# One layer of a hybrid attention and convolution trunk: the first two FFN groups' up products in another order around the last token tile, and one tile's block sums and one weight fetch a tile later

## The chip, the cores and the metric

The kernel runs on one core of a Trainium2 chip. The metric is device time in microseconds (us) of one execution, the median of several runs.

## The reference

One layer over 1024 tokens of 1024 channels, everything in float32. What matters here is the end of the mixer and the start of the feed-forward part:

```
m = sigmoid(g_att) * y_att + sigmoid(g_conv) * y_conv
x = x + rms_norm(m @ w_out, norm_mix_post)              # output projection
h = rms_norm(x, norm_ffn_pre)
a, g = split(causal_dwconv3(h @ w_up, conv_ffn_w))      # w_up: 1024 x 5632
x = x + rms_norm((gelu_tanh(g) * a) @ w_down, norm_ffn_post)
```

## The kernel before, in words

All matrix products run in float16 pairs: a float32 operand is split into a high and a low half (ACT writes the high half, L97, and VectorE the low half, L98), and three passes high·high, high·low and low·high are added up in PSUM. Before a weight is split, a power-of-two scale is made from its sum of squares: ACT squares it (L58, tile `jk_u2_0` for the first weight of group 2), VectorE reduces and casts (L70, L71), TensorE adds over partitions with a matrix of ones (L76, tile `pr`), and VectorE turns the result into the scale (L78 to L81, tile `sc`).

**Output projection** (mixer, L1112 to L1192). It goes over eight token tiles tt of 128 tokens. For each, `out_proj(tt)` issues 48 matmuls of 128x512 on PE (L1123, two PSUM banks `py`); ACT squares each bank for the norm (L1125, `jk_n_post`), VectorE takes it out (L1126, `hn`), then follow the row factor (L181 on VectorE, a power on POOL L182), the residual `x2` (L1130) and its write to memory by SP (L1131), a second square sum on ACT (L58, `jk_n_ffn`), again L181 and L182, and L1133 writes the normed row tile `hn`. The x rows `xr` come in by SP (L1176), one tile ahead, into a pool of 4 buffers that is shared with the raw FFN weights `ws_u`.

**Block sums** (`blocks(tt, h)`, L1136 to L1171). PE transposes `hn` in 8 steps into two banks `pt` (L1141). For tiles 0 to 3, ACT and VectorE only split them into `hA` (L1149, L1150). For tiles 4 to 7 they also build sums and differences of the four 512x512 blocks of h (L1155 to L1167, tiles `tb`, `hb`, into `hA` and `hB`).

**Up products** (class `Pair`). Each of the 22 groups f has the columns of w_up for 128 channels of a and of g. A 2x2 block product is done with seven block products instead of eight (a Strassen form), from four weight tiles `wh_u` and the blocks of hA and hB. `prod(i)` issues 12 matmuls of 128x512 (L1538) into one of three banks, and `evict` takes the sum out. Products 1 and 2 share bank a: product 1 is taken out by ACT (L1553, `cgu`), and product 2 adds on top of it in the same bank and is taken out as `cau` (L1603). Products 6, 7, 4 share bank b (L1555, L1562, L1567 on VectorE), products 5 and 3 bank c (L1558 on ACT, L1565 on VectorE). After product 3 and 4 come the convolutions (L1612 to L1615), the gelu (L1622) and the product `ua` (L1623).

```
    A = {1: (0, 0), 2: (0, 1), 3: (3, 0), 4: (1, 1), 5: (2, 0), 6: (2, 1), 7: (1, 0)}
        ...
        bank = {1: "a", 2: "a", 5: "c", 3: "c"}.get(i, "b")
        first = i in (1, 6, 5)
        if first:
            self.ps[bank] = l.bank(f"p{self.name}{bank}")
        ...
        with l.tc.high_priority():
            self.evict(i, ps)
```

Products 1 and 2 read hA of tokens 0 to 511 (tiles 0 to 3) alone. Products 5, 6 and 7 read hB, and products 3 and 4 the second half of hA, so they need the block sums of tile 7. `pu0a` is bank a of group 0, `pu1c` bank c of group 1, and so on.

**What sets the order.** The program is written in one order, and a scheduler of the framework moves instructions on each engine by its own simulated times, with priority for `evict` and, in the first two groups, for `blocks(7)`. PSUM is one pool of 8 banks. Engines execute their own instructions strictly in the resulting order. `pair_fetch` issues the two transfers of a group's weights and the square sums on ACT; `pair_sums` and `pair_split` build and split the four weight tiles (L1233 to L1248, L97, L98). The down product of FFN groups 0 and 1 (`pd`, L1312) needs the split gelu output `f16` and w_down tiles `wd`, which SP fetches (L1275) into the same pool of 4 raw weight buffers once a `ws_u` is split.

Of the kernel before, what the change touches and what calls it, by code (L numbers as in the profile page):

```python
# [39 lines left out]
class Layer:  # L40
# [235 lines left out]
    def mixer(self, mid):  # L276
# [716 lines left out]
        with ExitStack() as ph2:  # L993
# [8 lines left out]
            def blocks(q):  # L1002
                lo, hi = ds(0, NH), ds(NH, NH)
                kA, kB = ds(2 * q, 2), ds(KH + 2 * q, 2)

                def diff(name, p, m, hT_m=True):

                    t = self.slot([P, 2, NH], F32, f"{name}_{q}")
                    nc.vector.tensor_tensor(t, hT[:, 0, p[0], p[1]], hT[:, 0, m[0], m[1]] if hT_m else m,
                                            ALU.subtract)  # L1010
                    nc.vector.tensor_tensor(t, t, hT[:, 1, p[0], p[1]], ALU.add)
                    if hT_m:
                        nc.vector.tensor_tensor(t, t, hT[:, 1, m[0], m[1]], ALU.subtract)
                    return t
                t1 = diff("T1", (kA, hi), (kA, lo))
                halves(hB[:, :, 0, ds(2 * q, 2), :], t1)
                t2 = diff("T2", (kB, hi), t1, False)
                halves(hB[:, :, 1, ds(2 * q, 2), :], t2)
                t4s.append(diff("T4", (kB, lo), t2, False))
                t3 = diff("T3", (kB, hi), (kA, hi))  # L1020
                halves(hB[:, :, 2, ds(2 * q, 2), :], t3)
# [91 lines left out]
        def out_proj(tt):  # L1113
            xt = xr.pop(tt)
            sm = self.small(f"r_post{tt}")
            h = self.slot([P, D], F32, f"hn{tt}")
            jk = self.junk(f"jk_n_post{tt}")
            for nh in range(2):
                ps = self.bank(f"py{tt}_{nh}")
                sl = ds(nh * NH, NH)  # L1120
                for k in range(8):
                    for p, (hi, wi) in enumerate(PASSES):
                        nc.tensor.matmul(ps, m16[k][:, hi, ds(tt * P, P)], wo[k][:, wi, sl],  # L1123
                                         start=k == 0 and p == 0, stop=k == 7 and p == 2)
                nc.scalar.activation(jk[:, sl], ps, AF.Square, scale=sgn[:, 24:25], accum_out=sm[:, 3 + nh:4 + nh])  # L1125
                nc.vector.scalar_tensor_tensor(h[:, sl], ps, sgn[:, 24:25], gp[:, sl], ALU.mult, ALU.mult)  # L1126
            nc.vector.tensor_tensor(sm[:, 0:1], sm[:, 3:4], sm[:, 4:5], ALU.add)
            r = self.rstd(sm)
            y = self.xp.tile([P, D], F32, tag="x", name=f"x2_{tt}")
            nc.vector.scalar_tensor_tensor(y, h, r, xt, ALU.mult, ALU.add)  # L1130
            nc.sync.dma_start(self.x2[tt], y)  # L1131
            r2 = self.rstd_of(y, f"ffn{tt}")
            nc.vector.scalar_tensor_tensor(h, y, r2, gf, ALU.mult, ALU.mult)  # L1133
            return h
# [39 lines left out]
        def load_xr(tt):  # L1174
            xr[tt] = self.ws.tile([P, D], F32, tag="ws", name=f"xr{tt}")
            nc.sync.dma_start(xr[tt], a["x"][ds(tt * P, P), :])  # L1176

        hs = {}
        load_xr(0)
        for tt in range(8):  # L1180
            if tt + 1 < 8:
                load_xr(tt + 1)
            hs[tt] = out_proj(tt)
            if tt == 0:
                self.pair_split("u0")
                self.pair_fetch("u1")
            if tt == 3:
                self.pair_sums("u1")
                self.pair_split("u1")
            if tt == 4:  # L1190
                self.pair_fetch("u2")
            for t in {2: (0,), 3: (1,), 4: (2,), 5: (3, 4), 6: (5,), 7: (6,)}.get(tt, ()):  # L1192
                blocks(t, hs[t])
        self.pairs = {f: Up(self, f) for f in range(NFF)}
        p0, p1 = self.pairs[0], self.pairs[1]
        p0.prod(1)
        p1.prod(1)
        p0.prod(2)
        with tc.high_priority():
            blocks(7, hs[7])  # L1200
        p1.prod(2)
        p0.prod(5)
        p1.prod(5)

    def dn_sums(self, n):

# [461 lines left out]
```

## Time and profile before

| | |
|---|---|
| time, median of 3 runs | 1352.25 us (1351.61 to 1354.85) |
| profiled execution, time | 1350.92 us |
| profiled execution, span | 1349.2 us |
| PE busy | 1311.9 us, 97% |
| VectorE (DVE) busy | 1050.8 us, 78% |
| ACT busy | 859.1 us, 64% |
| output projection on PE | 616.4 to 705.1 us |
| first up product on PE | 706.63 us |
| first down product on PE | 786.24 us |

A row of the timeline reads: start, length, engine, line, operation, tile written <- tiles read, shape, count; in square brackets how long the engine stood idle before it, and what ended that. Matmuls overlap in the pipeline, so a row of 12 matmuls that lasts 2.75 us is followed by the next 2.59 us after its start.

### The profile page before, as it was taken

To read this page: it belongs to the slowest core of one execution; us is meant where nothing else is said; L and a number is where in the kernel's file an instruction comes from. 1 tells how busy PE (TensorE), PEld (TensorE's weight loads), DVE (VectorE), ACT (ScalarE), POOL (GpSimd) and SP (SyncE) were. 2 spreads that over 40 slices of the span, in tenths; PEclk is the share of its full clock that TensorE was granted. 3 is DMA by queue.
4 is the path that set the end of the run, shared out by engine and by line. 5 is a ranking of instruction groups with operands and counts; after the bars stand their busy time and mean duration, and the time that the engine had idled before them with its cause. 6 is when DMAs were issued, how large, how long until landed. Compare 5 with 4: busy or idle time off the path is not lost. (4 is left out here: it accounts for less than half of the span.)

```text
span 1349.2 us, 16783 instructions
## 1 busy us (share of the span) xinstructions
PE 1311.9 (97%) x6491; PEld 590.0 (44%) x6491; DVE 1050.8 (78%) x1697; ACT 859.1 (64%) x1205; POOL 34.5 (3%) x58
## 2 busy tenths in 40 slices
PE   5999999999998999999999999999999999999997
PEld 3544444344433444444444444444444444444443
DVE  6568887878878957878788977975894896699855
ACT  6578877877777966665555676743752762576524
POOL 2000000000000000000110000000000000000002
PEclk9999999999999999999999999999999999999999
DMA  7011201101001222241431123222220312313126
GB/s 267 33 33 32 63 32 32 36 28 48 32 16 32 63 63 66 76 177 57 137 114 44 51 63 126 63 63 94 63 94 1 125 63 63 125 34 123 63 48 109
DMA packets 26608, 96.12 MB, mean 71 GB/s; under 512 B 3088, under 2 KB 3216, under 8 KB 26528
## 3 DMA queue, kind: packets, MB, share of 16 engines
q1 hardware_dynamic: 25088, 89.80, 20.2%
q0 software_dynamic: 1440, 5.24, 2.1%
q8 instruction: 51, 0.84, 0.3%
q14 instruction: 29, 0.24, 0.1%
HBM read 86.61 MB, written 8.42 MB: 70 GB/s over the span
## 5 line engine op out<-in xcount | busy, mean ns | idle before, releaser
L1538 PEld LDWEIGHTS <-wh_u 128*128 128x128 f16 x1848 | 178.8, 98 | 217.6 <-issue 3.8
L1312 PE MATMUL pd<-wdh,f 128*128 128x512 f16 (+1 forms) x1068 | 230.2, 377 | 2.7 <-ACT wdh L97 1.1
L1312 PEld LDWEIGHTS <-f 128*128 128x128 f16 x1068 | 104.5, 98 | 126.9 <-issue 4.0
L97 ACT ACTIVATE wh_u<-ws_u,sc 128x1024 f16<-128x1024 f32 (+1 forms) x66 | 64.7, 999 | 103.6 <-DVE sc L80 80.0
L1319 DVE SCALAR_TENSOR_TENSOR yacc<-pd,sd,yacc 128x512 f32<-128x512 f32 (+1 forms) x81 | 58.6, 742 | 73.4 <-PE pd L1312 65.9
L1538 PEld LDWEIGHTS <-wh_g 128*128 128x128 f16 x588 | 56.9, 98 | 68.7 <-issue 0.4
L1123 PE MATMUL py<-wh_wo,m 128*128 128x512 f16 x384 | 83.9, 379 | 0.0
L98 DVE SCALAR_TENSOR_TENSOR wh_u<-ws_u,sc,wh_u 128x1024 f16<-128x1024 f32 (+1 forms) x66 | 72.4, 1103 | 9.5 <-ACT wh_u L97 9.4
L824 ACT ACTIVATE sh<-sp 128x1024 f16<-128x1024 f32 (+3 forms) x48 | 40.4, 841 | 53.4 <-DVE sp L819 53.1
L1615 DVE SCALAR_TENSOR_TENSOR ugu<-cgu,cw_g,ugu 128x1023 f32<-128x1023 f32 (+1 forms) x44 | 56.4, 1283 | 11.3 <-ACT ugu L1613 10.9
L828 DVE TENSOR_TENSOR sh<-sp,sh 128x1024 f16<-128x1024 f32 (+3 forms) x48 | 45.9, 956 | 18.0 <-ACT sh L824 17.8
L1615 DVE SCALAR_TENSOR_TENSOR ua<-cau,cw_a,ua 128x1023 f32<-128x1023 f32 (+1 forms) x44 | 56.3, 1280 | 1.4 <-ACT ua L1613 1.3
L1123 PEld LDWEIGHTS <-m 128*128 128x128 f16 x384 | 37.5, 98 | 44.1
L819 DVE TENSOR_TENSOR sp<-A,sp 1x1024 f32<-1x1024 f32 (+3 forms) x40 | 35.9, 897 | 25.4 <-PE A L781 21.7
L850 ACT ACTIVATE w<-e 128x1024 f16<-128x1024 f32 (+3 forms) x48 | 40.5, 843 | 21.3 <-DVE e L845 20.4
L854 DVE SCALAR_TENSOR_TENSOR w<-e,w 128x1024 f16<-128x1024 f32 (+3 forms) x48 | 45.8, 954 | 9.2 <-ACT w L850 9.2
L814 ACT ACTIVATE sp<-e,one 128x1024 f32<-128x1024 f32 (+3 forms) x48 | 44.4, 925 | 6.0 <-DVE e L809 3.1
L845 DVE TENSOR_TENSOR e<-e,g 128x1024 f32<-128x1024 f32 (+3 forms) x48 | 45.7, 953 | 1.9 <-ACT g L841 1.8
L58 ACT ACTIVATE jk_u<-ws_u 128x1024 bf16<-128x1024 f32 x44 | 46.4, 1054 | 0.8
L756 PE MATMUL pywc<-p,wh_wc 128*128 128x512 f16 x192 | 43.2, 379 | 3.5 <-ACT sga L730 1.1
L211 PE MATMUL pcb<-hT,wh_cb 128*128 128x512 f16 x192 | 44.9, 379 | 0.9 <-DVE sc_cb L89 0.8
L800 ACT ACTIVATE e<-z,cz 128x1024 f32<-128x1024 f32 (+3 forms) x48 | 43.0, 897 | 3.6 <-PE z L781 3.6
(697 smaller groups left out, 2623.3 us busy)
## 6 DMA issues: line engine op xcount, KB each, us to landing
ws_u<-w_up_nt SPq DMA_DIRECT2D x44, 512.0 KB
ds<-w_down SPq DMA_DIRECT2D x22, 512.0 KB
wd<-w_down SPq DMA_DIRECT2D x22, 512.0 KB
ws_g<-w_in_nt SPq DMA_DIRECT2D x14, 512.0 KB
x<-x SPq DMA_DIRECT2D x8, 512.0 KB
ws_wo<-w_out SPq DMA_DIRECT2D x8, 512.0 KB
xr<-x SPq DMA_DIRECT2D x8, 512.0 KB
out<-x SPq DMA_DIRECT2D x7, 512.0 KB
```

Source lines behind the costliest of these rows:

```text
L58: self.nc.scalar.activation(self.junk(f"jk_{name}"), src, AF.Square, accum_out=acc)
L97: self.nc.scalar.activation(dst[:, 0, :], src, AF.Copy, scale=s)
L98: self.nc.vector.scalar_tensor_tensor(dst[:, 1, :], src, s, dst[:, 0, :], ALU.mult, ALU.subtract)
L211: nc.tensor.matmul(ps, w[:, wi, ds(k * P, P)], hT[:, hi, k, ds(c * NH, NH)], start=n == 0, stop=n == last)
L828: nc.vector.tensor_tensor(sh[:, 1, :, off:], u["sp"][:, :, off:], sh[:, 0, :, off:], ALU.subtract)
L845: nc.vector.tensor_tensor(e[:, :, off:], e[:, :, off:], u["g"][:, :, off:], ALU.mult)
L854: nc.vector.scalar_tensor_tensor(w[:, 1, :, off:], u["e"][:, :, off:], 2.0 ** 14, w[:, 0, :, off:], ALU.mult, ALU.subtract)
L1123: nc.tensor.matmul(ps, m16[k][:, hi, ds(tt * P, P)], wo[k][:, wi, sl], start=k == 0 and p == 0, stop=k == 7 and p == 2)
L1312: nc.tensor.matmul(pd[nh], f16[g][k][:, hi, ds(tt * P, P)], w[k][:, wi, ds(*part)], start=run is runs[0] and n == 0, stop=run is runs[-1] ...
L1319: nc.vector.scalar_tensor_tensor(y[:, sl], ps, sm[:, 0:1], y[:, sl], ALU.mult, ALU.add)
L1538: nc.tensor.matmul(ps, w[wt][:, wi, ds(wc * NH + k * P, P)], self.block(i, hi, k), start=first and n == 0, stop=n == 3 * KH - 1, skip_grou ...
L1615: nc.vector.scalar_tensor_tensor(u[:, lag:], c[:, :T - lag], sm[:, 2 - lag:3 - lag], u[:, lag:], ALU.mult, ALU.add)
```

## The change

The sums of tile 1 are called after the projection of tile 4 instead of 3, with those of tile 2; the weights of group 2 are fetched after tile 5 instead of 4; and around tile 7 the first products stand in another order: group 0's product 2 ahead of group 1's product 1, and product 5 of group 1 ahead of that of group 0. The tuple `order` lists the tiles in the order they had. One line is added, so line numbers behind L1178 are one higher in the changed kernel.

```
         hs = {}
-        load_xr(0)
+        order = (0, 1, 2, 3, 4, 5, 6, 7)
+        load_xr(order[0])
         for tt in range(8):
             if tt + 1 < 8:
-                load_xr(tt + 1)
-            hs[tt] = out_proj(tt)
+                load_xr(order[tt + 1])
+            hs[order[tt]] = out_proj(order[tt])
             if tt == 0:
                 self.pair_split("u0")
                 self.pair_fetch("u1")
             if tt == 3:
                 self.pair_sums("u1")
                 self.pair_split("u1")
-            if tt == 4:
+            if tt == 5:
                 self.pair_fetch("u2")
-            for t in {2: (0,), 3: (1,), 4: (2,), 5: (3, 4), 6: (5,), 7: (6,)}.get(tt, ()):
+            for t in {2: (0,), 4: (1, 2), 5: (3, 4), 6: (5,), 7: (6,)}.get(tt, ()):
                 blocks(t, hs[t])
         self.pairs = {f: Up(self, f) for f in range(NFF)}
         p0, p1 = self.pairs[0], self.pairs[1]
         p0.prod(1)
+        p0.prod(2)
         p1.prod(1)
-        p0.prod(2)
         with tc.high_priority():
             blocks(7, hs[7])
         p1.prod(2)
+        p1.prod(5)
         p0.prod(5)
-        p1.prod(5)
```

What the scheduler makes of it is seen in the engines' orders, of which three places matter.

On PE, around the transposes `pt7` of the last token tile; `pu0a` and `pu1a` are the banks of products 1 and 2 of groups 0 and 1, and of each run of 12 equal matmuls one is shown. Before:

```order
L1538 MATMUL pu0a_6439<-hA_5641,wh_u0_0_5738 128x512
...
L1538 MATMUL pu1a_6455<-hA_5641,wh_u1_0_6000 128x512
...
L1141 MATMUL pt7_0_6484<-ident_80,hn7_6340 128x128 x4
L1141 MATMUL pt7_1_6485<-ident_80,hn7_6340 128x128 x4
L1538 LDWEIGHTS wh_u0_2_5740
L1538 MATMUL pu0c_6528<-hB2_5642,wh_u0_2_5740 128x512
```

And now:

```order
L1539 MATMUL pu0a_6439<-hA_5641,wh_u0_0_5738 128x512
...
L1141 MATMUL pt7_0_6484<-ident_80,hn7_6340 128x128 x4
L1141 MATMUL pt7_1_6485<-ident_80,hn7_6340 128x128 x4
L1539 LDWEIGHTS wh_u1_0_6000
L1539 MATMUL pu1a_6468<-hA_5641,wh_u1_0_6000 128x512
...
L1539 MATMUL pu1c_6528<-hB2_5642,wh_u1_2_6002 128x512
```

The transposes of tile 7 have moved ahead of the 12 matmuls of product 2 of group 1; those now stand between the transposes and the first product that reads hB. In front, the run is product 1 of group 0, product 1 of group 1, product 2 of group 0 in both kernels.

On ACT, from the second norm of tile 4 to the block sums of tile 4 (`jk_u2_0`, `jk_u2_1` are the square sums of group 2's weights, `jk_n_post5` that of tile 5's projection), before and then now:

```order
L58 ACTIVATE jk_n_ffn4_6093,r_ffn4_6092<-x2_4_6089 128x1024
L58 ACTIVATE jk_u2_0_6101,sm_u2_6098<-ws_u2_0_6099 128x1024
L58 ACTIVATE jk_u2_1_6105,sm_u2_6098<-ws_u2_1_6103 128x1024
L1125 ACTIVATE jk_n_post5_6125,r_post5_6123<-py5_0_6126,sgn_564 128x512
L1125 ACTIVATE jk_n_post5_6125,r_post5_6123<-py5_1_6153,sgn_564 128x512
```

```order
L58 ACTIVATE jk_u2_0_6186,sm_u2_6183<-ws_u2_0_6184 128x1024
L1155 ACTIVATE hA_5641<-hb4_6225 128x4x128
L1155 ACTIVATE hA_5641<-tb4_1_6217 128x4x128
L58 ACTIVATE jk_u2_1_6190,sm_u2_6183<-ws_u2_1_6188 128x1024
L1155 ACTIVATE hB2_5642<-tb4_1_6217 128x4x128
L1125 ACTIVATE jk_n_post6_6241,r_post6_6239<-py6_0_6242,sgn_564 128x512
```

The two square sums have moved from ahead of tile 5's norm into the block sums of tile 4, ahead of tile 6's norm.

On VectorE, behind the last block sum of tile 7 (`cau0` is the sum of product 6 taken out of bank b of group 0, `sc18` the scale of group 2's weights, made from `pr19`), before and then now:

```order
L1156 TENSOR_TENSOR hB2_5642<-tb7_1_6495,hB2_5642 128x4x128
L1555 TENSOR_TENSOR cau0_6452<-pu0b_6564,cgu0_6453 128x512
L1565 TENSOR_TENSOR cau0_6452<-pu0c_6528,cau0_6452 128x512
L78 TENSOR_SCALAR sc18_6628<-pr19_6632 128x1
L1233 TENSOR_TENSOR s12_u2_6611<-ws_u2_1_6103 128x512
```

```order
L78 TENSOR_SCALAR sc18_6628<-pr19_6632 128x1
L80 TENSOR_SCALAR sc18_6628<-sc18_6628 128x1
L81 TENSOR_SCALAR sc18_6628<-sc18_6628 128x1
L98 SCALAR_TENSOR_TENSOR wh_u2_0_6637<-ws_u2_0_6184,sc18_6628,wh_u2_0_6637 128x1024
L1556 TENSOR_TENSOR cau0_6452<-pu0b_6564,cgu0_6453 128x512
L1566 TENSOR_TENSOR cau0_6452<-pu0c_6543,cau0_6452 128x512
L1556 TENSOR_TENSOR cau1_6481<-pu1b_6668,cgu1_6482 128x512
```

The scale and the first split of group 2's weights have moved ahead of the first sums that are taken out of banks b and c. From the down product of groups 0 and 1 on, all engines' orders are the same again but for a few neighbours that change places.

More of the change, by code (lines that the diff above doesn't have):

```diff
@@ L1178, in mixer @@
         hs = {}
-        load_xr(0)
+        order = (0, 1, 2, 3, 4, 5, 6, 7)
+        load_xr(order[0])
         for tt in range(8):
             if tt + 1 < 8:
-                load_xr(tt + 1)
-            hs[tt] = out_proj(tt)
+                load_xr(order[tt + 1])
+            hs[order[tt]] = out_proj(order[tt])
             if tt == 0:
@@ L1189, in mixer @@
                 self.pair_split("u1")
-            if tt == 4:
+            if tt == 5:
                 self.pair_fetch("u2")
-            for t in {2: (0,), 3: (1,), 4: (2,), 5: (3, 4), 6: (5,), 7: (6,)}.get(tt, ()):
+            for t in {2: (0,), 4: (1, 2), 5: (3, 4), 6: (5,), 7: (6,)}.get(tt, ()):
                 blocks(t, hs[t])
@@ L1196, in mixer @@
         p0.prod(1)
+        p0.prod(2)
         p1.prod(1)
-        p0.prod(2)
         with tc.high_priority():
@@ L1201, in mixer @@
         p1.prod(2)
+        p1.prod(5)
         p0.prod(5)
-        p1.prod(5)
     def dn_sums(self, n):
```

## The prediction

> **What bounds the kernel now.** I read the page first, then busy times by stage, then the timeline around the end of the output projection. The page says that TensorE is nearly always at work:
>
> ```profile
> span 1349.2 us, 16783 instructions
> PE 1311.9 (97%) x6491; PEld 590.0 (44%) x6491; DVE 1050.8 (78%) x1697; ACT 859.1 (64%) x1205; POOL 34.5 (3%) x58
> ```
>
> By stage (columns: stretch, its length, busy us and instructions of PE, weight loads, VectorE, ACT, POOL, then granted clock, DMA share, GB/s):
>
> ```profile
> 640.00:706.00 66.00, 65.37 (x329) 32.54 (x328) 54.82 (x94) 39.65 (x78) 10.42 (x14) 1.00 0.38 128
> 706.00:722.00 16.00, 12.98 (x67) 6.50 (x66) 14.81 (x29) 10.90 (x20) 1.60 (x2) 1.00 0.20 67
> 722.00:740.00 18.00, 18.00 (x87) 8.19 (x86) 12.73 (x21) 8.08 (x11) 0.00 (x0) 1.00 0.01 1
> 740.00:784.00 44.00, 44.00 (x209) 20.00 (x208) 40.82 (x68) 29.96 (x38) 0.00 (x0) 1.00 0.19 60
> 784.00:800.00 16.00, 14.32 (x67) 6.36 (x65) 14.45 (x18) 8.50 (x13) 0.00 (x0) 1.00 0.34 99
> ```
>
> The change moves instructions between about 659 and 800 us and adds or removes none. TensorE's work stays the same, so only its gaps can change: 0.63 us in the first stretch, 3.02 in the second, 1.68 in the last, 5.33 in all. Their places on PE:
>
> ```profile
> 705.70 1.09 PE L1141 MATMUL pt<-ident,hn 128*128 128x128 f32 x8 [0.63 <-DVE hn L1133]
> 706.63 2.75 PE L1538 MATMUL pu0a<-hA,wh_u 128*128 128x512 f16 x12
> 709.22 2.75 PE L1538 MATMUL pu1a<-hA,wh_u 128*128 128x512 f16 x12
> 712.99 2.75 PE L1538 MATMUL pu0a<-hA,wh_u 128*128 128x512 f16 x12 [1.02 <-ACT cgu L1553]
> 715.58 2.75 PE L1538 MATMUL pu1a<-hA,wh_u 128*128 128x512 f16 x12
> 718.17 1.04 PE L1141 MATMUL pt<-ident,hn 128*128 128x128 f32 x8
> 721.00 0.38 PE L1538 MATMUL pu0c<-hB,wh_u 128*128 128x512 f16 x1 [1.79 <-ACT hB L1155]
> 721.79 2.54 PE L1538 MATMUL pu0c<-hB,wh_u 128*128 128x512 f16 x11 [0.20 <-DVE hB L1156]
> 788.93 0.38 PE L1312 MATMUL pd<-wdh,f 128*128 128x512 f16 x1 [1.03 <-DVE cau L1565]
> 789.96 4.04 PE L1312 MATMUL pd<-wdh,f 128*128 128x512 f16 x18 [0.65 <-ACT wdh L97]
> ```
>
> The 1.79 us gap is the largest. Product 5 needs the sums of tile 7, the transposes of tile 7 were issued at 718.17, and nothing stood between them and product 5. Equal runs of 12 matmuls start 2.59 us apart (706.63, 709.22), and the 8 transposes take 0.93 us of PE (705.70 to 706.63).
>
> **Term 1, the transposes of tile 7 ahead of product 2 of group 1.** These rows hold what they need and what follows:
>
> ```profile
> 714.40 0.58 ACT L1553 ACTIVATE cgu<-pu1a 128x512 f32<-128x512 f32 x1
> 715.10 1.28 DVE L1133 SCALAR_TENSOR_TENSOR hn<-x,r_ffn,g_ffn 128x1024 f32<-128x1024 f32 x1
> 716.96 0.58 ACT L1603 ACTIVATE cau<-pu0a 128x512 f32<-128x512 f32 x1
> 717.50 0.15 DVE L70 TENSOR_REDUCE sc<-sm_u 128x1 f32<-128x2 f32 x1
> 718.81 0.75 DVE L1157 SCALAR_TENSOR_TENSOR tb<-pt,g_ffn,hA 128x512 f32<-128x512 f32 x1 [0.97 <-PE pt L1141]
> ```
>
> Product 2 of group 0 keeps its place behind product 1 of group 1, and its wait for `cgu` (1.02 us) stays: on this point the edit in the source changes nothing. It starts at 712.99 and PE is free at 715.58. The row tile of tile 7 is done at 715.10 + 1.28 = 716.38, so PE now waits about 0.85 us for it, and the transposes end at about 717.3. Product 2 of group 1 then needs `cgu` of its bank. That eviction has moved on ACT from ahead of the last sums of tile 6 to behind `cau` of group 0: without it in front, `cau` starts about 0.5 us earlier, at 716.5, and `cgu` follows at 717.0 to 717.6. PE waits another 0.3 us and runs product 2 from 717.6 to 720.2. Meanwhile VectorE takes tile 7 out right behind its reduce, at about 717.57 instead of 718.81, since it no longer waits for PE. So both halves of hB are there 1.24 us earlier, at 719.76 and 720.55, and PE, which reaches product 5 at 720.2 and has two matmuls before it needs the second half, waits no more. Gone: 1.79 + 0.20. New: 0.85 + 0.3. Net gain 0.84 us. Bounds: 0 if the eviction of `cgu` is held up by the weights that ACT squares just ahead of it, 1.99 if both new waits vanish.
>
> The row factor on which the 716.38 hangs takes longer at some places than at others:
>
> ```profile
> L182 POOL TENSOR_TENSOR r_ffn<-r_ffn,neghalf x8: 549/550/2066, 644.7 to 713.7; 128x1 f32<-128x1 f32 x8
> 690.18 2.07 POOL L182 TENSOR_TENSOR r_ffn<-r_ffn,neghalf 128x1 f32<-128x1 f32 x1 [3.81 <-DVE r_ffn L181]
> 713.74 1.05 POOL L182 TENSOR_TENSOR r_ffn<-r_ffn,neghalf 128x1 f32<-128x1 f32 x1 [4.13 <-DVE r_ffn L181]
> ```
>
> The same operation takes 0.55 us mostly, 2.07 in tile 5 and 1.05 in tile 7. VectorE's order around it is the same in both kernels, so I keep 1.05. The Trainium skill ("SBUF — State Buffer", section "SBUF: two separate sides") says that GpSimd and a VectorE instruction with two SBUF inputs lock each other out for a whole instruction; the long rows agree, since such instructions surround them. By that rule a request that comes a moment later sits out one more of them, which by an estimate from the 0.69 us of such rows would add about 0.6 us to the new wait and leave about 0.2 of term 1.
>
> **Term 2, the later sums and the later fetch.** Before, the two square sums stood ahead of tile 5's norm:
>
> ```profile
> 679.56 1.06 ACT L58 ACTIVATE jk_u<-ws_u 128x1024 bf16<-128x1024 f32 x1
> 680.74 1.06 ACT L58 ACTIVATE jk_u<-ws_u 128x1024 bf16<-128x1024 f32 x1
> 682.78 1.42 DVE L1126 SCALAR_TENSOR_TENSOR hn<-py,sgn,g_post 128x512 f32<-128x512 f32 x2 [0.52 <-ACT jk_n_post L1125]
> ```
>
> VectorE waited 0.52 us for that norm and then took out both halves of tile 5 in a row, after gaps of 1.28 and 0.66 us before the second normed tile:
>
> ```profile
> 679.51 0.15 DVE L181 TENSOR_SCALAR r_ffn<-r_ffn 128x1 f32<-128x1 f32 x1 [1.28 <-ACT jk_n_ffn L58]
> 680.33 1.28 DVE L1133 SCALAR_TENSOR_TENSOR hn<-x,r_ffn,g_ffn 128x1024 f32<-128x1024 f32 x1 [0.66 <-POOL r_ffn L182]
> ```
>
> Now the first half goes into those gaps, so VectorE is 0.52 + 0.67, about 1.1 us ahead at tile 4's sums. ACT then has two square sums more there (1.18 us from one to the next), and VectorE the reduce and cast (about 0.15 us); that takes back some 0.4 us at tile 6's norm. About 0.6 us of lead remain for the chain to `hn` of tile 6, on which PE waited 0.63 us. I take 0.5 (bounds: -0.4, should the square sums delay tile 6's norm, and 0.63). The sums of tile 1 take the same time later: VectorE has the gaps above for them, and the 8 transposes of tile 1 cost PE the same 0.9 us behind tile 4 as behind tile 3. SP now has tile 6's rows ahead of the two weight transfers and `x2` of tile 3 ahead of tile 5's rows; their users come 10 us later, so that is hidden, and would cost a transfer's 3.5 us (below) if it weren't.
>
> **Term 3, the down product of groups 0 and 1.**
>
> ```profile
> 729.33 0.69 DVE L1555 TENSOR_TENSOR cau<-pu0b,cgu 128x512 f32<-128x512 f32 x1 [3.37 <-PE pu0b L1538]
> 731.92 0.69 DVE L1565 TENSOR_TENSOR cau<-pu0c,cau 128x512 f32<-128x512 f32 x1 [1.90 <-PE pr L76]
> 784.47 0.75 DVE L98 SCALAR_TENSOR_TENSOR wh_u<-ws_u,sc,wh_u 128x512 f16<-128x512 f32 x1
> 788.76 1.15 ACT L97 ACTIVATE wdh<-wd,sc 128x1024 f16<-128x1024 f32 x1 [2.16 <-DMA wd<-w_down]
> ```
>
> The last wait ends on a chain: the split at 784.47 frees the buffer at 785.2, the transfer lands at 788.76 (3.5 us), ACT splits for 1.15 us, PE goes on at 789.96. So VectorE sets this point. It was idle for 3.37 + 1.90 us at 726 to 732; now the first split of group 2 (1.28 us) falls there, but the eviction of bank c behind it is awaited until about 733.0, since PE's order has 10 matmuls of bank b more ahead. Followed at these durations VectorE comes to 784 ahead by somewhat more than PE; I take 0.4 us off the 1.68 (bounds: 1.68 at best, and a loss in the first rival).
>
> Sum: 0.84 + 0.5 + 0.4 = 1.74 us. The profiled execution took 1350.92 us (1349.2 of span), 1.33 less than the median of 1352.25, just below the three runs' 1351.61 to 1354.85. Taken off it: 1349.2; off the median: 1350.5.
>
> **The rivals.** *VectorE becomes the bound and the down product waits longer.* Between 729.2 and 733.0 VectorE would stand 3.8 us before an eviction with the whole queue of splits behind it. If the stages after it, 40.82 of 44 us busy, make nothing good, the point at 789.96 comes 3.8 - 1.4 = 2.4 us later (1.4: the split and the three scale steps done before). Time 1354.6; it decides as soon as VectorE comes to 784 later than before, since PE has no other work ready there. At worst, all of the 3.8 us and a little more: 1356.3. For it: the share of 93%. Against it: VectorE had gaps to make it good in.
>
> ```profile
> 760.73 1.23 DVE L1623 TENSOR_TENSOR ua<-ugu,ua 128x1024 f32<-128x1024 f32 x1 [1.86 <-ACT ugu L1622]
> 775.65 1.28 DVE L1615 SCALAR_TENSOR_TENSOR ugu<-cgu,cw_g,ugu 128x1023 f32<-128x1023 f32 x1 [0.70 <-ACT ugu L1613]
> ```
>
> The Trainium skill ("TensorE: Matmul & The Clock Gate", section "HAM oscillation — how this bites in real kernels") says that a PE gap over about 3.4 us halves the array's clock for a while; no gap here shows it (3.02 us in pieces at 706 to 722, clock 1.00). By that rule this rival's gap would cost an estimated 1.7 us more.
>
> *The gain is given back.* Terms 1 and 2 bring PE to the down product sooner and it waits there for the same VectorE and DMA chain: 0, 1352.2. For it: the wait's end does not depend on PE directly. Against: VectorE's chain starts from PE's evictions at 729.
>
> *All gaps close.* If also `cgu` comes early enough, up to 5.33 us go: 1346.9. Against: the orders around `cgu` are unchanged.
>
> **How the numbers follow.** Forecast 0.45, the gain given back 0.25, VectorE as the bound 0.15, all gaps close 0.15. The likeliest gives 1350.5. One in ten stays out on each side: low 1348.2, inside the last case, high 1354.0, near the first rival's 1354.6. 0.3% is 4.05 us, about what a measurement of this kernel can tell from no change. A gain of more takes over three quarters of 5.33: 0.11 of the last case's 0.15. A loss of more takes the first rival's worst end: 0.06. The rest, 0.83, is within.
>
> **What would show it.** In the changed kernel's timeline: right, if the 8 transposes of `pt7` stand ahead of the second `pu1a` with a wait near 0.85 us on `hn`, product 2 waits some 0.3 us on `cgu`, and `pu1c` has no wait; if the wait on `hn` of tile 6 is below 0.63; and if `pd`'s waits sum to about 1.3. Wrong, if `pu1a` waits over 1 us on `cgu`, if PE's down product starts its 18 matmuls later than 789.96, or if PE shows a gap between 722 and 784, where it had none.

## The result and the profile after

The changed kernel takes 1348.32 us (median of 8 runs, 1347.04 to 1349.36), the kernel before 1351.65 us (8 runs, 1350.38 to 1354.85). The ratio on record is 0.9972, with a 95% interval of 0.9962 to 0.9982; the two medians alone give 0.9975. Each run below has its ratio to the kernel before as measured in the same session. The profiled execution took 1348.23 us, with a span of 1346.5 us. So the kernel is faster, as forecast, but by about twice the forecast 1.74 us.

The page of the changed kernel shows as many instructions as before:

```profile
span 1346.5 us, 16783 instructions
PE 1313.1 (98%) x6491; PEld 590.3 (44%) x6491; DVE 1050.4 (78%) x1697; ACT 859.2 (64%) x1205; POOL 34.5 (3%) x58
```

Busy times by stage, in the stretches and columns of the prediction:

```profile
640.00:706.00 66.00, 66.00 (x334) 33.09 (x333) 55.32 (x95) 39.73 (x78) 10.42 (x14) 1.00 0.37 128
706.00:722.00 16.00, 13.82 (x70) 6.69 (x68) 15.86 (x32) 12.89 (x24) 1.60 (x2) 1.00 0.20 67
722.00:740.00 18.00, 18.00 (x86) 8.12 (x85) 11.62 (x20) 7.25 (x10) 0.00 (x0) 1.00 0.01 1
740.00:784.00 44.00, 44.00 (x209) 20.04 (x208) 43.09 (x72) 31.33 (x40) 0.00 (x0) 1.00 0.21 61
784.00:800.00 16.00, 15.67 (x74) 6.96 (x73) 12.92 (x14) 9.56 (x16) 0.00 (x0) 1.00 0.30 96
```

PE's gaps in the first two and the last stretch are now 0, 2.18 and 0.33 us, 2.51 in place of 5.33. VectorE is busy for 43.09 of the 44 us ahead of the down product, where it was busy for 40.82. The places on PE:

```profile
705.47 1.09 PE L1141 MATMUL pt<-ident,hn 128*128 128x128 f32 x8
712.78 2.75 PE L1539 MATMUL pu0a<-hA,wh_u 128*128 128x512 f16 x12 [1.04 <-ACT cgu L1554]
716.29 1.06 PE L1141 MATMUL pt<-ident,hn 128*128 128x128 f32 x8 [0.77 <-DVE hn L1133]
717.74 2.75 PE L1539 MATMUL pu1a<-hA,wh_u 128*128 128x512 f16 x12 [0.38 <-ACT cgu L1554]
720.75 2.54 PE L1539 MATMUL pu1c<-hB,wh_u 128*128 128x512 f16 x11
787.42 4.04 PE L1313 MATMUL pd<-wdh,f 128*128 128x512 f16 x18 [0.33 <-ACT wdh L97]
```

The waits of 0.63, 1.79, 0.20 and 1.03 us are gone. The two new ones are 0.77 on `hn` and 0.38 on `cgu`, close to the 0.85 and 0.3 forecast. What comes before the output projection varies by up to 2.5 us from one profile to the next (last section), so I measure from the first `py` matmul of the output projection (616.64 us before, where the table ahead has 616.4, and 617.27 after) and split the rest at three marks: the transposes `pt6`, the run of 11 matmuls of product 5, and the run of 18 matmuls of `pd`. The table has this for all kernels that could be split so, from the same rows of each timeline, and the busy time of VectorE from 740 to 784 us:

| kernel | `py` to `pt6` | to product 5 | to `pd` x18 | to the end | sum | DVE 740 to 784 |
|---|---|---|---|---|---|---|
| before | 89.06 | 16.09 | 68.17 | 559.24 | 732.56 | 40.82 |
| changed | 88.20 | 15.28 | 66.67 | 559.08 | 729.23 | 43.09 |
| run 1: sums and fetch only | 88.21 | 16.08 | 68.20 | 559.01 | 731.50 | 40.83 |
| run 2: product order only | 89.05 | 15.32 | 66.62 | 559.00 | 729.99 | 43.10 |
| run 3: run 2, product 5 as before | 89.05 | 15.38 | 68.64 | 559.33 | 732.40 | 39.32 |
| run 5: before, no gelu wait | 89.04 | 16.08 | 66.88 | 559.27 | 731.27 | 41.75 |
| run 6: changed, no gelu wait | 88.21 | 15.31 | 66.74 | 559.02 | 729.28 | 43.04 |
| run 7: fetch only | 88.31 | 16.03 | 68.02 | 559.06 | 731.42 | 40.83 |
| run 9: two small steps earlier | 88.96 | 15.16 | 66.75 | 558.98 | 729.85 | 43.10 |

The changed kernel gains 0.86, 0.81, 1.50 and 0.16 us, in all 3.33. The marks repeat from profile to profile to within 0.2 us where a stage's order is the same, which is finer than the interval of a ratio (0.001 is 1.35 us).

The second new wait, 0.38 on `cgu`, hangs on ACT's order: the second square sum of group 3's weights starts at 715.56 there, and `cau` (716.62) and `cgu` (717.10) follow behind it; run 10 tests this.

The third gain, 1.50 us, is the one that the prediction had too small. The split of `wh_u4_3`, which frees the buffer for the down product's weights, moved from 784.47 to 781.96. Before, one step stood in VectorE's queue between the last convolution and the product with the gelu, and another wait came about 5 us later:

```profile
758.17 0.69 DVE L1567 TENSOR_TENSOR cgu<-pu1b,cgu 128x512 f32<-128x512 f32 x1
760.73 1.23 DVE L1623 TENSOR_TENSOR ua<-ugu,ua 128x1024 f32<-128x1024 f32 x1 [1.86 <-ACT ugu L1622]
...
765.44 1.28 DVE L1615 SCALAR_TENSOR_TENSOR ugu<-cgu,cw_g,ugu 128x1023 f32<-128x1023 f32 x1 [0.58 <-ACT ugu L1613]
```

Here is VectorE in the changed kernel:

```profile
753.81 1.28 DVE L1616 SCALAR_TENSOR_TENSOR ugu<-cgu,cw_g,ugu 128x1022 f32<-128x1022 f32 x1
755.00 1.28 DVE L98 SCALAR_TENSOR_TENSOR wh_u<-ws_u,sc,wh_u 128x1024 f16<-128x1024 f32 x1
756.20 0.69 DVE L1249 TENSOR_TENSOR ws_u<-ws_u,s_u 128x512 f32<-128x512 f32 x1
756.80 1.28 DVE L98 SCALAR_TENSOR_TENSOR wh_u<-s_u,sc,wh_u 128x1024 f16<-128x1024 f32 x1
757.99 1.22 DVE L1624 TENSOR_TENSOR ua<-ugu,ua 128x1024 f32<-128x1024 f32 x1
...
762.01 0.69 DVE L1566 TENSOR_TENSOR cau<-pu2c,cau 128x512 f32<-128x512 f32 x1 [0.56 <-PE pu2c L1539]
...
772.40 0.69 DVE L1556 TENSOR_TENSOR cau<-pu3b,cgu 128x512 f32<-128x512 f32 x1 [0.23 <-PE pu3b L1539]
...
781.96 0.74 DVE L98 SCALAR_TENSOR_TENSOR wh_u<-ws_u,sc,wh_u 128x512 f16<-128x512 f32 x1
```

and what ACT does meanwhile:

```profile
755.16 1.28 ACT L1623 ACT_TABLE_LOAD   x1 [0.32 <-DVE ugu L1616]
756.46 1.06 ACT L1623 ACTIVATE ugu<-ugu 128x1024 f32<-128x1024 f32 x1
```

After the last convolution of group 0's gate, ACT needs 1.28 us to load a table and 1.06 us for the gelu. In the changed kernel three steps of group 3 stand in VectorE's queue at this place and fill the time; before they stood ahead of the last convolution, and VectorE waited. Its waits between 733 us and the split of `wh_u4_3` sum to 0.56 + 0.23 = 0.79 us after, and to 1.86 + 0.58 + 0.70 = 3.14 before.

### The profile page after: what moved, and what is told of

Its sections match the earlier page's. It is cut to its first block, busy times and chain, and to the rows that moved or that the text cites. A ratio compares the mean times of both kernels' runs of the same rounds, so it can differ in the third digit from the quotient of the medians.

```text
span 1346.5 us, 16783 instructions
## 1 busy us (share of the span) xinstructions
PE 1313.1 (98%) x6491; PEld 590.3 (44%) x6491; DVE 1050.4 (78%) x1697; ACT 859.2 (64%) x1205; POOL 34.5 (3%) x58
## 4 chain that ended last, share of the span: by engine, by line
PE 62%; DVE 4%; ACT 1%; issue 1%; DMA 1%; POOL 0%; POOLq 0%; DVEq 0%; SPq 0%; ACTq 0%
PE pd L1313 16%; PE py L1123 5%; PE pywa L756 3%; PE pywc L756 2%; PE pu18b L1539 1%; PE pu14b L1539 1%; PE pu11b L1539 1%; PE pu16b L1539 1%; PE pg5b L1539 1%; PE pu20b L1539 1%; PE pu12b L1539 1%; PE pu10b L1539 1%; PE pu8b L1539 1%; PE pu7b L1539 1%; PE pu6b L1539 1%
```

## The experiments

The theory: three gains that do not depend on each other. The later fetch ends the wait ahead of `pt6` (0.86), the place of `pt7` shortens the waits around it (0.81), and VectorE's order behind tile 7, which comes with the order of the products, brings the down product forward, chiefly because work stands in the queue where the gelu was waited for (1.50). The rivals: the 1.50 come from the later fetch; or from the transposes being earlier; or the parts work only together. All kernels are edits of the changed kernel, or of the changed kernel with its order set back to that of before.

**Run 1, sums and fetch only.** The products are set back to the order of before:

```
         p0.prod(1)
-        p0.prod(2)
         p1.prod(1)
+        p0.prod(2)
 ...
-        p1.prod(5)
         p0.prod(5)
+        p1.prod(5)
```

> Only the sums of tile 1 and the fetch of group 2 are later; the products stand in the order of the kernel before. Theory (three separate gains: 0.8 us ahead of tile 6's transposes, 0.8 around tile 7's, 1.5 at the down product, the last from VectorE's order that comes with the product order): no wait ahead of pt6, the 1.02, 1.79 and 0.20 waits around pt7 and the 1.03 and 0.65 at the down product all there; 0.8 us less than before, ratio 0.9994. Rival 1 (the gain at the down product comes from the later fetch, which moves work off the engines there): 2.3 us less, ratio 0.9983. Rival 2 (what is gained at pt6 is given back at the down product): no difference, 18 matmuls of pd at 789.9 again.

Measured: 1351.06 us, ratio 0.9993 (0.9984 to 1.0002). On PE:

```profile
704.71 1.09 PE L1141 MATMUL pt<-ident,hn 128*128 128x128 f32 x8
...
720.00 0.38 PE L1539 MATMUL pu0c<-hB,wh_u 128*128 128x512 f16 x1 [1.79 <-ACT hB L1155]
...
788.99 4.04 PE L1313 MATMUL pd<-wdh,f 128*128 128x512 f16 x18 [0.69 <-ACT wdh L97]
```

The interval reaches 1, so the reading rests on the marks. The `pt6` wait is gone and nothing else. The 0.85 us from `py` to `pt6` last to the end although the waits at the down product stay (68.20 against 68.17), so rival 2 falls: the VectorE chain that ends there starts from PE and moves with it. Rival 1 falls too.

**Run 2, product order only.** Sums and fetch set back:

```
-            if tt == 5:
+            if tt == 4:
                 self.pair_fetch("u2")
-            for t in {2: (0,), 4: (1, 2), ...
+            for t in {2: (0,), 3: (1,), 4: (2,), ...
```

> Only the product order is changed; tile 1's sums and the fetch of group 2 stand where they were before. VectorE's order behind tile 7 is then that of the changed kernel word for word. Theory of three separate gains: the pt6 wait of 0.63 is there again, the waits around pt7 are those of the changed kernel, 66.7 us from the first pu1c after the wait (or pu0c) to the 18 matmuls of pd; 2.3 us less than before, ratio 0.9983. Rival 1 (the gain at the down product hangs on the later fetch): 0.8 us less, ratio 0.9994. Rival 2 (the parts only work together): within 0.3 us of before.

Measured: 1348.59 us, ratio 0.9978 (0.9969 to 0.9987):

```profile
707.76 1.09 PE L1141 MATMUL pt<-ident,hn 128*128 128x128 f32 x8 [0.63 <-DVE hn L1133]
...
718.58 1.06 PE L1141 MATMUL pt<-ident,hn 128*128 128x128 f32 x8 [0.76 <-DVE hn L1133]
...
789.70 4.04 PE L1313 MATMUL pd<-wdh,f 128*128 128x512 f16 x18 [0.29 <-ACT wdh L97]
```

The `pt6` wait is back, and the second and third gain are there in full (15.32 and 66.62). By the traces runs 1 and 2 gain 1.06 and 2.57 us, 3.63 together against 3.33 for both at once: the parts add up, but for 0.3 us.

**Run 3, product 5 of group 0 first again.** Run 2 with the last two products exchanged:

```
-        p1.prod(5)
         p0.prod(5)
+        p1.prod(5)
```

> As the run with the product order alone, but product 5 of group 0 stays ahead of that of group 1: the transposes of tile 7 still move ahead of product 2 of group 1, and VectorE's order behind is a third one, in which the third group's four splits stand ahead of the last convolution and nothing is queued between that and the product with the gelu. Theory (the 1.5 us at the down product come from work queued on VectorE to cover the gelu of group 0): 0.8 us of gain around pt7, a VectorE wait of over 1 us on the gelu as before, down product as late as before relative to product 5 (about 68 us), in all 0.8 us less than before, ratio 0.9994. Rival (they come from the transposes being earlier, or from group 2's first split being ahead): 2.3 us less, ratio 0.9983.

Measured: 1351.67 us, ratio 0.9999 (0.9990 to 1.0008). VectorE's wait on the gelu:

```profile
761.40 1.23 DVE L1624 TENSOR_TENSOR ua<-ugu,ua 128x1024 f32<-128x1024 f32 x1 [2.46 <-ACT ugu L1623]
```

The gain around `pt7` is there (15.38), the wait on the gelu is even longer than before, and the down product comes 2.0 us later than in run 2 (68.64 against 66.62), 0.6 later than the theory said. Group 2's first split stands ahead in this order too, and `pt7` is as early as in run 2. So neither of them alone brings the 1.50 us, and the rival falls.

**Run 4, only product 5 exchanged.** Of the order of before, with sums and fetch as before:

```
-        p0.prod(5)
         p1.prod(5)
+        p0.prod(5)
```

> Only product 5 of group 1 ahead of that of group 0; products 1 and 2 and the transposes of tile 7 stand as before. VectorE then has a split of group 3 and a sum of bank b between the last convolution of group 0's gate and the product with the gelu. Theory (cover of the gelu): the waits around pt7 as before (1.02, 1.79, 0.20), no gain there; the gelu wait on VectorE below 0.6 us, and about 1 us gained at the down product: 1 us less than before, ratio 0.9993. Rival (the transposes' place gives both gains): no difference from before.

Measured: 1352.34 us, ratio 1.0007 (0.9998 to 1.0015). The theory missed here:

```profile
762.63 1.23 DVE L1624 TENSOR_TENSOR ua<-ugu,ua 128x1024 f32<-128x1024 f32 x1 [1.20 <-ACT ugu L1623]
```

```profile
790.84 0.38 PE L1313 MATMUL pd<-wdh,f 128*128 128x512 f16 x1 [1.04 <-DVE cau L1566]
792.03 2.53 PE L1313 MATMUL pd<-wdh,f 128*128 128x512 f16 x11 [0.82 <-DVE wdh L98]
794.91 2.53 PE L1313 MATMUL pd<-wdh,f 128*128 128x512 f16 x11 [0.35 <-ACT wdh L97]
```

The two steps between the convolution and the product cover less than I had counted: 1.20 us of waiting are left, and behind it the orders of groups 3 and 4 are others too, with a new wait for VectorE's split of `wdh`. The profiled execution also lost 1.48 us to a lower clock right behind product 5 (last section), so its later marks can't be set beside the others and the time decides: no gain. The exchange of product 5 gains only together with the earlier `pt7`. What the scheduler makes of both is the cause, not either line of the edit.

**Runs 5 and 6, the gelu wait taken away.** To test the wait itself, group 0's gelu writes to a scratch tile, so the output lacks that gelu, in the order of before (run 5) and in the changed kernel (run 6):

```
-        nc.scalar.activation(ug, ug, AF.Gelu_apprx_tanh)
+        gl = l.junk("jk_gelu") if self.f == 0 else ug
+        nc.scalar.activation(gl, ug, AF.Gelu_apprx_tanh)
         nc.vector.tensor_tensor(self.ua, ug, self.ua, ALU.mult)
```

> The order of the kernel before, and for group 0 alone the gelu's result goes into a scratch tile: VectorE's product behind it reads the gate without the gelu and so doesn't wait for ACT (the kernel leaves that gelu out of its output). All instructions and their lengths stay. Theory (the gelu wait of 1.86 us on VectorE is what makes the down product late): the waits around pt7 as before, the gelu wait gone, the split of wh_u4_3 1.3 to 1.9 us earlier relative to product 5, the waits of 1.03 and 0.65 at pd down to 0.4 in all; 1.3 us less than before, ratio 0.9990. Rival 1 (VectorE next waits for TensorE's sums of group 2, so the time is lost there): wh_u4_3 as late as before, no difference. Rival 2 (the earlier first split of group 2 is what counts): no difference either.

> The same edit in the changed kernel (group 0's gelu left out of the output; all engines' orders are those of the changed kernel). Theory: its gelu wait is hidden behind three splits already, so nothing is gained but at most the 0.33 us left at pd: ratio to before 0.9974 to 0.9977, as the changed kernel. Rival (the edit itself makes a kernel faster, whatever the order): 1 us or more less than the changed kernel, ratio 0.9965.

Measured: run 5 1350.04 us, ratio 0.9990 (0.9982 to 0.9999); run 6 1347.82 us, ratio 0.9970 (0.9959 to 0.9981). VectorE in run 5, and below it ACT and PE:

```profile
761.15 0.69 DVE L1563 TENSOR_TENSOR cgu<-pu2b,cgu 128x512 f32<-128x512 f32 x1 [0.90 <-PE pu2b L1539]
...
783.69 0.75 DVE L98 SCALAR_TENSOR_TENSOR wh_u<-ws_u,sc,wh_u 128x512 f16<-128x512 f32 x1
```

```profile
787.73 1.15 ACT L97 ACTIVATE wdh<-wd,sc 128x1024 f16<-128x1024 f32 x1 [1.63 <-DMA wd<-w_down]
788.93 4.04 PE L1313 MATMUL pd<-wdh,f 128*128 128x512 f16 x18 [0.34 <-ACT wdh L97]
```

And PE in run 6:

```profile
786.78 4.04 PE L1313 MATMUL pd<-wdh,f 128*128 128x512 f16 x18 [0.40 <-ACT wdh L97]
```

Without the gelu wait the kernel before has its down product 1.29 us earlier (66.88 against 68.17), and the wait of 1.03 us there is gone, as in the changed kernel. 0.90 us of the wait return at the next sum, and still the split of `wh_u4_3` is 1.04 us earlier: 61.64 us behind product 5 (783.69 - 722.05), against 62.68 (784.47 - 721.79). The other 0.25 us lie behind the split: the second `wd` tile lands sooner, so that ACT's split of it starts 4.04 us after that of `wh_u4_3`, where it was 4.29 before and 4.26 in the changed kernel; why is open. The same edit does nothing in the changed kernel (66.74 against 66.67). So the gelu wait costs the kernel before most of the third gain: 1.04 of the 1.47 us at the split, and with the earlier landing 1.29 of the 1.50 at the down product; the changed kernel is rid of it by order alone. In run 5 some steps behind the product change places as well, so the figures are not quite those of the wait alone.

**Run 7, the fetch only.** Of the order of before, only the fetch of group 2's weights is later:

```
-            if tt == 4:
+            if tt == 5:
                 self.pair_fetch("u2")
```

> Only the fetch of group 2's weights is a tile later; tile 1's sums and the products stand as before. Theory (the pt6 wait goes because the two square sums leave ACT's queue ahead of tile 5's norm): no wait ahead of pt6, 0.6 to 0.8 us less, ratio 0.9994. Rival (it is tile 1's sums, which make room on VectorE and PE): the 0.63 wait is there, no difference.

Measured: 1350.11 us, ratio 0.9992 (0.9983 to 1.0001):

```profile
704.59 1.04 PE L1141 MATMUL pt<-ident,hn 128*128 128x128 f32 x8
```

The interval reaches 1 here too, so the marks decide: no wait ahead of `pt6`, and 88.31 us up to it. So the first gain is the fetch's; the later sums of tile 1 add at most 0.1 us (88.31 to 88.21).

**Run 8, tile 7 first.** Can the rest of the waits around `pt7` go too? The changed kernel with tile 7's projection at raised priority:

```
-            hs[order[tt]] = out_proj(order[tt])
+            with (tc.high_priority() if tt == 7 else __import__('contextlib').nullcontext()):
+                hs[order[tt]] = out_proj(order[tt])
```

> The changed kernel with tile 7's projection and norm at raised priority, to bring its row tile earlier: the half of tile 5's transposes falls behind tile 7's matmuls, and pt7 moves ahead of product 2 of group 0. If tile 7's row tile is what still costs 0.77 us of PE and the 1.04 us on cgu can be covered by pt7, up to 1.5 us less than the changed kernel, ratio to before 0.9965. Rival (VectorE is full from 702 to 724 us, so what tile 7 gains the sums of tiles 5 and 6 lose, and products 5 come no earlier): ratio 0.9975 or above.

Measured: 1358.04 us, ratio 1.0048 (1.0036 to 1.0060):

```profile
717.61 1.94 PE L1141 MATMUL pt<-ident,hn 128*128 128x128 f32 x8 [6.75 <-DVE hn L1133]
```

```profile
706.00:722.00 16.00, 9.26 (x38) 4.71 (x37) 15.97 (x31) 10.37 (x19) 1.38 (x2) 0.80 0.20 66
```

Both expectations were too kind. `pt7` now stands ahead of product 2 of group 0, VectorE is busy for 15.97 of the 16 us and brings tile 7's row tile no earlier (its transposes start 101.13 us after the first `py`, 99.02 in the changed kernel), and PE has nothing else in its order for 6.75 us. Its granted clock is down to 0.80 in this stretch.

**Run 9, two small steps earlier.** The convolution weights `cw_a0` and `cw_g0` of group 0, two VectorE steps that stood ahead of tile 7's row tile, are made after tile 1:

```
+            if tt in (1, 4):
+                self.cw_early(tt // 4)
 ...
```

`cw_early` makes the two weights of group 0 and does nothing for other groups.

> The changed kernel, with two small VectorE instructions of group 0 (convolution weights cw_a0 and cw_g0) computed some tiles earlier, so that they no longer stand ahead of tile 7's row tile; TensorE's order and the rest of VectorE's stay. Theory (of the two new waits around pt7 the second, on cgu of group 1, ends by ACT's order alone): hn of tile 7 is 0.2 to 0.4 us earlier, pt7's wait falls from 0.77 to about 0.4, the wait on cgu grows from 0.38 by the same amount, nothing gained: ratio to before as the changed kernel, 0.9972 to 0.9977. Rival (tile 7's row tile sets it): 0.2 to 0.4 us less than the changed kernel.

Measured: 1349.10 us, ratio 0.9983 (0.9974 to 0.9992). The POOL step behind tile 7's row factor and VectorE's answer, then PE:

```profile
712.87 1.65 POOL L182 TENSOR_TENSOR r_ffn<-r_ffn,neghalf 128x1 f32<-128x1 f32 x1 [3.94 <-DVE r_ffn L181]
```

```profile
714.56 1.28 DVE L1133 SCALAR_TENSOR_TENSOR hn<-x,r_ffn,g_ffn 128x1024 f32<-128x1024 f32 x1 [0.44 <-POOL r_ffn L182]
```

```profile
715.99 1.07 PE L1141 MATMUL pt<-ident,hn 128*128 128x128 f32 x8 [0.93 <-DVE hn L1133]
717.35 2.75 PE L1552 MATMUL pu1a<-hA,wh_u 128*128 128x512 f16 x12 [0.29 <-ACT cgu L1567]
```

The request to POOL comes earlier, and POOL takes 1.65 us for it, not 1.05: `hn` is no earlier relative to `pt6` (9.35 us behind it, 9.40 in the changed kernel). So the expected shift did not take place, and which of the two waits binds stays untested. 0.12 us are won around `pt7`; another wait of 0.60 us at 682.71, at an earlier tile's transposes, costs more.

**Run 10, group 3's second square sum later as well.** In run 9, the square sum that stands ahead of `cau` and `cgu` on ACT is issued behind product 6 of group 1:

```
-            self.sumsq(t, sm[:, i:i + 1], f"{name}_{i}")
+            if name == "u3" and i in (1,):
 ...
+            else:
+                self.sumsq(t, sm[:, i:i + 1], f"{name}_{i}")
 ...
                 p.prod(6)
+                self.late((f, 'p6'))
```

> As the run before, and the second square sum of group 3's weights (1.06 us on ACT ahead of cau and cgu) later. Around pt7 both waits should now shrink, together from 1.15 to 0.5 us or less: 0.6 us gained there. But the scheduler then makes group 3's splits later throughout: nothing covers the gelu of group 0, and four splits of groups 3 and 4 come close together ahead of the down product. Theory (VectorE's order between 733 and 784 us decides the down product): the gain at the down product is lost again or more, slower than the changed kernel by 1 us or more, ratio to before 0.9980 or above. Rival (what is won at tile 7 stays): 0.6 us less than the changed kernel, ratio 0.9968.

Measured: 1358.66 us, ratio 1.0056 (1.0042 to 1.0070):

```profile
712.47 2.75 PE L1562 MATMUL pu0a<-hA,wh_u 128*128 128x512 f16 x12 [0.67 <-ACT cgu L1577]
716.14 1.07 PE L1150 MATMUL pt<-ident,hn 128*128 128x128 f32 x8 [0.91 <-DVE hn L1142]
759.29 0.19 PE L76 MATMUL pr<-rb,ones 128*128 128x1 bf16 x1 [8.37 <-DVE rb L71]
```

Around `pt7` the wait on `cgu` of group 1 is gone, so it was this square sum that it hung on. The wait on `hn` is 0.91, not smaller as expected, but that on `cgu` of group 0 fell to 0.67, and the stage from `pt6` to product 5 takes 14.51 us in place of 15.28, about the gain expected. But in PE's order the single small matmul that adds up group 3's square sum stands ahead of the next products and holds them for 8.37 us: the late square sum now comes behind group 0's gelu on ACT (at 756.86). The sign of the expectation was right, the place and the size were not: it is this matmul on PE, not the down product.

## Why the prediction was right and wrong

**Term 1, around `pt7`, was right:** 0.84 us forecast, 0.81 measured (0.77 in run 2). Both new waits came where they were said to, within 0.1 us of the values given, and VectorE takes tile 7 out at 717.34, where 717.57 was forecast.

**Term 2, the fetch, was right in its mechanism and too small:** 0.5 forecast, bound 0.63, measured 0.86. The bound of 0.63 was itself too low: the row of `py` ahead of the wait overlaps with what follows when nothing waits, so `pt6` now starts 10.39 us after that row, where it started 11.15 after it, 0.76 in all. The remaining 0.10 lie ahead of that row. VectorE's two takings-out of tile 5 lie where they were forecast, but the wait of 0.52 us on tile 5's norm stays, now ahead of the second half. The lead was 0.96 us at tile 4's sums, near the forecast 1.1 (whose 0.52 + 0.67 is 1.19). Of the 0.4 us that the square sums were to take back at tile 6's norm, 0.13 came: the lead is 0.98 at `hn` of tile 5 and 0.85 at `hn` of tile 6.

**Term 3, the down product, is the step that failed:** 0.4 forecast, 1.50 measured, close to its upper bound of 1.68. It holds 1.10 of the 1.59 us by which the forecast 1.74 fell short of 3.33. I followed VectorE's work from 732 to 784 us with the waits it had before, and counted only that it starts later and has 1.4 us less to do. In the trace it starts 1.15 us later (733.07 against 731.92), has 1.31 us less to do, and waits 2.35 us less (0.79 against 3.14): 2.51 in all, of which PE, itself 1.04 us earlier, sees 1.47 at the split of `wh_u4_3`. The term left out, 2.35, is larger than the two counted. Those two alone, 1.4 less the later start of about 1.1, bring the split 0.3 us earlier, while PE was to come 1.34 us earlier by terms 1 and 2; so the 0.4 us did not follow from them, and that its sign was right is luck as far as the working shows. The row with the wait of 1.86 us on the gelu was quoted, but as room in which VectorE could make good a loss; that the changed order might fill it was to be read in VectorE's order, some 30 rows behind those shown.

**The rivals.** VectorE did stand for 3.67 us ahead of an eviction, as the rival with VectorE as the bound had it (3.8), but the loss did not come: VectorE reaches the split 1.47 us earlier relative to product 5. The gain given back fell in run 1. That all gaps close came half true, since the gaps on PE fell from 5.33 to 2.51 us.

## What to carry to other kernels

When an in-order engine's queue decides a point downstream, follow its new order row by row up to that point and ask of each wait in it whether something stands in the queue ahead of it now; its old waits are not a constant. A change of order that pays should be split into its parts on the chip: here each half of the product order was worth nothing by itself, and both together 2.6 us. Near such a point small edits (two steps of 0.28 us, one square sum) can cost more than they bring, so the whole order has to be looked at, not the line that was edited.

## What the runs showed of the hardware

The same 3.05 us gap of PE, at about 408 to 411 us and far from the change, is followed by slow matmuls in some executions and not in others. Before, and then after:

```profile
411.20 1.16 PE L781 MATMUL A<-sh,tri 128*128 128x512 f16 x4 [3.04 <-ACT g L841]
```

```profile
411.78 1.86 PE L781 MATMUL A<-sh,tri 128*128 128x512 f16 x4 [3.05 <-ACT g L841]
```

In 6 of the 12 profiles the granted clock from 404 to 420 us is below 1.00 (0.89 in the changed kernel, 0.79 in run 2). Run 2 is 0.43 us behind the kernel before when this gap ends (411.63 against 411.20), and 2.07 us behind at its first `py`. In run 4 it happened behind tile 7 as well, where PE ran only the transposes and two matmuls between 718.22 and 721.84:

```profile
721.84 4.02 PE L1539 MATMUL pu1c<-hB,wh_u 128*128 128x512 f16 x11 [0.20 <-DVE hB L1156]
```

That is 1.48 us more than the 2.54 of the same run elsewhere. The Trainium skill ("TensorE: Matmul & The Clock Gate", section "HAM oscillation — how this bites in real kernels") names gaps of more than about 3.4 us as the ones that throttle. These traces differ from it: a gap of 3.04 to 3.05 us was followed by a lower clock in half of the profiles. The prediction had the profile of the kernel before alone, in which it was not. Before the first `py` all kernels have the same instructions, so what happens there is a spread between executions and no part of the change's gain. The lower clock behind tile 7 is another matter: the kernel before and runs 1, 5 and 7 have the same waits there and a clock of 1.00 in their one profile each, and the changed kernel no longer has these waits. Whether some other executions of the kernel before lose time there, which would add to the gain of the medians, no profile shows.

On POOL, the Trainium skill ("SBUF — State Buffer", section "SBUF: two separate sides") lets an instruction of VectorE with two inputs in SBUF and GpSimd shut each other out. Run 9 agrees: a request that came 0.4 us earlier (7.66 us behind `pt6`, 8.05 in the changed kernel) took 1.65 us where it had taken 1.05, and behind it VectorE's two instructions of 0.69 us (712.83, 713.43) follow each other directly, where one of 0.28 us stood between them in the changed kernel (714.08). The 0.6 us more are what the prediction estimated for a request that sits out one more such instruction.
